# One load-and-store queue, two orders: store, load per tile against two stores, two loads per pair of tiles, with a new start and end

## The chip, the cores and the metric

One core of one Trainium2 chip. The metric is the device time of the kernel in microseconds (us). The time before was 4976.5 us, the median of three runs (4975.0 to 4977.91). The record lists a granted clock of 1.00 for every run and the state of all of them as fast.

Two kinds of engine appear below. VectorE and ScalarE compute. The 16 DMA engines move data. In the trace of the kernel before, a whole transfer is 128 packets of 64 KiB (32,512 for 254 whole transfers) and leaves 16 landings, up to 5.7 us apart, of which I take one for each DMA engine; the kernel waits for all 16 (near 2496 us the last came at 2496.28 and VectorE's first reduce began at 2496.36), so a transfer counts here as landed with the last. "Fastest" and "slowest" are the first and the last of these 16 to end a given transfer. The kernel allocates its tiles in SBUF, and a scratch tile that no transfer touches in PSUM.

## The reference

```python
# x: (256, 256, 4096) float32, eps = 1e-5
mean = np.mean(x, axis=2, keepdims=True)
var = np.var(x, axis=2, keepdims=True)
return ((x - mean) / np.sqrt(var + eps)).astype(np.float32)
```

That is 65,536 independent rows of 4,096 numbers, 1.07 GB in and 1.07 GB out. The inputs are drawn from a normal distribution, so they are nearly normalised already. A kernel that only copies x to out therefore passes the tolerance of the comparison.

## The kernel before

A tile is 128 partitions with 4 rows each: 8.39 MB per transfer, 128 tiles, three buffers. All transfers go through one queue (q1 alone on the page, with 37,152 packets), fed by SyncE in program order.

```python
    P, K, BUFS, C = 128, 4, 3, 64
    X = [pool.tile([P, K, d], fp32, name=f"x{s}") for s in range(BUFS)]
    ...
    def take(engine, sem, count):
        engine.wait_ge(sem, count)
        engine.sem_clear(sem)
    ...
    def store(s, k, dst):                      # waits until the tile is computed
        take(S, done[s], k)
        S.dma_start(out=dst, in_=X[s][:, :k, :]).then_inc(stored[s], 16)

    def load(s, k, src):                       # waits until the buffer is stored
        take(S, stored[s], 16)
        S.dma_start(out=X[s][:, :k, :], in_=src).then_inc(loaded[s], 16)
    ...
            def _(sync):
                ...
                load(0, K, x_t[0])
                load(1, K, x_t[1])
                with S.Fori(0, rounds * BUFS, BUFS) as i:
                    for s in range(BUFS):
                        store(s, K, out_t[...i + s...])              # cut: the slice arithmetic
                        load((s + 2) % BUFS, K, x_t[...i + s + 2...])
                # cut: the last tiles; the last one is loaded and stored as two halves of 2 rows
```

Per row, VectorE reduces (mean), ScalarE squares with a running sum (variance), and the two share the work of applying scale and bias. All of a tile's rows must be through before its store is issued.

## Time and profile before

The prediction below shows the page, the stretches and the chain of this kernel. What else the argument needs:

| | before |
|---|---|
| median time, first 3 runs | 4976.5 us |
| span of the profiled execution | 4973.1 us |
| VectorE busy, ScalarE busy | 68%, 52% |
| last landing | 4971.72 us |
| slowest DMA engine, per transfer, 300-2300 us, 2500-4800 us | 19.369 us, 19.337 us |
| slowest behind fastest, near 2400 us, near 4650 us | 5.7 us, 4.9 us |

Two views of the kernel before, to be set against the changed one. First the long stretches (start:end, length, VectorE, ScalarE, POOL, clock, DMA share, GB/s):

```profile
300.00:2300.00 2000.00, 1369.43 (x982) 1049.92 (x604) 0.00 (x0) 1.00 1.00 434
2500.00:4800.00 2300.00, 1584.18 (x1137) 1210.90 (x695) 0.00 (x0) 1.00 1.00 434
```

Then the DMA issues (what, engine, count, KB each, median us from issue to landing), and the spread of that time for the stores' line:

```profile
x<-in_x_dram SPq DMA_DIRECT2D x127, 49.1
out_dram<-x SPq DMA_DIRECT2D x127, 30.4
```

```profile
DMA to landing us min/median/max: 13.8/30.4/35.1
```

A transfer takes 19.3 us. A store that lands 30.4 us after its issue was issued some 11 us before the transfer ahead of it was through. This is the reserve that keeps the queue fed; it matters below. I call it the store's **margin**: from the issue of the store to the moment at which a DMA engine ends the transfer before it. It is shorter on the fastest engine (about 6 us) than on the slowest (about 11 us), by the 5 to 6 us that lie between them.

### The profile page before, as it was taken

To read this page: it belongs to the slowest core of one execution; us is meant where nothing else is said; L and a number is where in the kernel's file an instruction comes from. 1 tells how busy PE (TensorE), PEld (TensorE's weight loads), DVE (VectorE), ACT (ScalarE), POOL (GpSimd) and SP (SyncE) were. 2 spreads that over 40 slices of the span, in tenths; PEclk is the share of its full clock that TensorE was granted. 3 is DMA by queue.
4 is the path that set the end of the run, shared out by engine and by line. 5 is a ranking of instruction groups with operands and counts; after the bars stand their busy time and mean duration, and the time that the engine had idled before them with its cause. 6 is when DMAs were issued, how large, how long until landed. Compare 5 with 4: busy or idle time off the path is not lost.

```text
span 4973.1 us, 6421 instructions
## 1 busy us (share of the span) xinstructions
DVE 3396.3 (68%) x2436; ACT 2599.6 (52%) x1493; POOL 0.2 (0%) x4
## 2 busy tenths in 40 slices
DVE  6666666677667776676666776677766766677766
ACT  5455554455545555455545555455554555455545
POOL 0000000000000000000000000000000000000000
DMA  9999999999999999999999999999999999999999
GB/s 380 434 432 432 434 431 434 433 434 434 435 434 434 433 435 434 434 434 433 435 431 438 431 436 433 434 434 433 435 432 436 432 436 431 433 435 432 434 434 411
DMA packets 37155, 2147.52 MB, mean 432 GB/s; under 512 B 4128, under 2 KB 4128, under 8 KB 4128
## 3 DMA queue, kind: packets, MB, share of 16 engines
q1 hardware_dynamic: 37152, 2147.50, 99.8%
q14 instruction: 3, 0.02, 0.0%
HBM read 1073.74 MB, written 1073.74 MB: 432 GB/s over the span
## 4 chain that ended last, share of the span: by engine, by line
DMA 74%; DVE 17%; ACT 7%; issue 1%; another core or an unknown queue 1%; SPq 0%; ACTq 0%; DVEq 0%
DMA x<-in_x_dram 42%; DMA out_dram<-x 32%; DVE part L87 16%; ACT junk L127 3%; ACT x L135 3%; DVE nsum L89 1%; DVE nmean L91 1%; DVE x L107 0%; ACTq L153 0%; SPq L141 0%; ACT std L132 0%; SPq L145 0%; ACTq L69 0%; ACT L119 0%
## 5 line engine op out<-in xcount | busy, mean ns | idle before, releaser
L87 DVE TENSOR_REDUCE part<-x 128x64 f32<-128x4096 f32 x512 | 2258.8, 4412 | 1438.2 <-DMA x<-in_x_dram 1438.2
L127 ACT ACTIVATE junk<-x,nmean 128x4096 f32<-128x4096 f32 x512 | 1882.2, 3676 | 2337.3 <-DVE nmean L91 2337.3
L107 DVE TENSOR_SCALAR x<-x,rstd,nbias 128x4096 f32<-128x4096 f32 x383 | 912.5, 2411 | 37.7 <-DVE nbias L99 16.0
L135 ACT ACTIVATE x<-x,nbias,rstd 128x4096 f32<-128x4096 f32 x129 | 488.5, 3787 | 0.0
L89 DVE TENSOR_REDUCE nsum<-part 128x1 f32<-128x64 f32 x512 | 112.7, 220 | 17.7
L127 ACT ACTIVATION_READ_ACCUMULATOR junk<-x,nmean 128x1 f32 x512 | 95.5, 187 | 0.0
L91 DVE TENSOR_SCALAR nmean<-nsum 128x1 f32<-128x1 f32 x512 | 78.7, 154 | 17.5
L97 DVE RECIPROCAL rstd<-std 128x3 f32<-128x3 f32 (+1 forms) x258 | 42.0, 163 | 39.9 <-ACT std L119 31.5
L127 ACT ACT_TABLE_LOAD x41 | 52.6, 1283 | 2.0 <-DVE eps_tile L177 1.2
L119 ACT ACT_TABLE_LOAD x41 | 52.6, 1283 | 0.7
L99 DVE TENSOR_TENSOR nbias<-nmean,rstd 128x3 f32<-128x3 f32 (+1 forms) x258 | 41.5, 161 | 8.9
L132 ACT ACTIVATE std<-ss,eps_tile 128x1 f32<-128x1 f32 x129 | 38.0, 295 | 15.0
L119 ACT ACTIVATE std<-ss,eps_tile 128x3 f32<-128x3 f32 x129 | 38.2, 296 | 3.3
L177 DVE MEMSET eps_tile<- 128x1 f32 x1 | 0.1, 59 | 1.0 <-SPq L152 1.0
L208 POOL MEMSET const-bfloat16-1.0<- 128x1 bf16 x1 | 0.1, 101 | 0.0
L208 POOL MEMSET const-uint8-127<- 128x1 uint8 x1 | 0.1, 101 | 0.0
L208 POOL MEMSET const-float32-0.0<- 128x1 f32 x1 | 0.1, 98 | 0.2 <-issue 0.2
L208 POOL MEMSET const-float32-1.0<- 128x1 f32 x1 | 0.1, 98 | 0.0
## 6 DMA issues: line engine op xcount, KB each, us to landing
x<-in_x_dram SPq DMA_DIRECT2D x2, 4096.0 KB, 29.6
out_dram<-x SPq DMA_DIRECT2D x2, 4096.0 KB, 17.4
x<-in_x_dram SPq DMA_DIRECT2D x127, 49.1
out_dram<-x SPq DMA_DIRECT2D x127, 30.4
```

Source lines behind the costliest of these rows:

```text
L87: mine(V.tensor_reduce(out=part[s][:, r, :], in_=row, axis=AX.X, op=ALU.add))
L89: mine(V.tensor_reduce(out=nsum[s][:, c], in_=part[s][:, r, :], axis=AX.X, op=ALU.add, negate=True))
L91: V.tensor_scalar_mul(out=nmean[s][:, c], in0=nsum[s][:, c], scalar1=1.0 / d).then_inc(means, 1)
L97: mine(V.reciprocal(out=rstd[s][:, c], in_=std[s][:, c]))
L99: mine(V.tensor_mul(out=nbias[s][:, c], in0=nmean[s][:, c], in1=rstd[s][:, c]))
L107: V.tensor_scalar(out=x[:, r, :], in0=x[:, r, :], scalar1=rstd[s][:, c], scalar2=nbias[s][:, c], op0=ALU.mult, op1=ALU.add,).then_inc(done ...
L119: A.activation(out=std[s][:, : k - 1], in_=ss[s][:, : k - 1], func=AF.Sqrt, bias=eps_tile, scale=1.0 / d).then_inc(stds, 1)
L127: A.activation(out=junk, in_=x[:, r, :], func=AF.Square, bias=nmean[s][:, c], scale=1.0, accum_out=ss[s][:, c]).then_inc(own_a, 1)
L132: A.activation(out=std[s][:, c], in_=ss[s][:, c], func=AF.Sqrt, bias=eps_tile, scale=1.0 / d).then_inc(stds, 1)
L135: A.activation(out=x[:, k - 2, :], in_=x[:, k - 2, :], func=AF.Identity, bias=nbias[s][:, c], scale=rstd[s][:, c]).then_inc(done[s], 1)
L177: V.memset(eps_tile, eps).then_inc(ready, 1)
L208: nc = _bacc.Bacc("TRN2", target_bir_lowering=False, num_devices=1)
```

## The change

The intent: issue more loads before the first store, so that no hole is left at the start; halve the changes of direction in the queue; and have the last tile's data early. The first tile is loaded, computed and stored in halves. The last tile is loaded whole, computed and stored in halves.

```diff
-                load(0, K, x_t[0])
-                load(1, K, x_t[1])
-                with S.Fori(0, rounds * BUFS, BUFS) as i:
-                    for s in range(BUFS):
-                        store(s, K, ...)
-                        load((s + 2) % BUFS, K, ...)
+                for h in range(2):
+                    r = half_of(h)
+                    S.dma_start(out=X[0][:, r, :], in_=x_t[0][:, r, :]).then_inc(second(loaded, 0, h), 16)
+                load(1, 1, wait=False)
+                load(2, 2, wait=False)
+                store_half(0, 0, 0)
+                store_half(0, 0, 1)
+                store(1, 1)
+                take(S, stored[BUFS], 16)
+                load(0, 3)
+                load(1, 4)
+                with S.Fori(0, 20) as i:
+                    for j in range(L0, L0 + 6, 2):
+                        for t in (j, j + 1):
+                            store(t % BUFS, (t, 6, 20, i))
+                        for t in (j + 3, j + 4):
+                            load(t % BUFS, (t, 6, 20, i))
+                for op, t in ((store, 122), (store, 123), (load, 125), (store, 124), (load, 126), (load, 127),
+                              (store, 125), (store, 126)):
+                    op(t % BUFS, t)
+                store_half(last % BUFS, last, 0)
+                store_half(last % BUFS, last, 1)
```

Cut: the row offset that lets the compute functions work on half a tile, and one more semaphore of each kind for second halves.

More of the change, by code (lines that the diff above doesn't have):

```diff
@@ L35 @@
     out_t = out_flat.rearrange("(t p k) d -> t p k d", p=P, k=K)
+    assert ntiles == 128
     half = K // 2
-    h0 = n - P * K
-    x_h = x_flat[h0:n, :].rearrange("(h p k) d -> h p k d", p=P, k=half)
-    out_h = out_flat[h0:n, :].rearrange("(h p k) d -> h p k d", p=P, k=half)
     pool = ctx.enter_context(tc.tile_pool(name="pool", bufs=1))
@@ L53 @@
     )
-    loaded = [nc.alloc_semaphore(f"loaded{s}") for s in range(BUFS)]
-    stored = [nc.alloc_semaphore(f"stored{s}") for s in range(BUFS)]
+    loaded = [nc.alloc_semaphore(f"loaded{s}") for s in range(BUFS + 1)]
+    stored = [nc.alloc_semaphore(f"stored{s}") for s in range(BUFS + 1)]
     own_v = nc.alloc_semaphore("own_v")
@@ L63 @@
     scaled = nc.alloc_semaphore("scaled")
-    done = [nc.alloc_semaphore(f"done{s}") for s in range(BUFS)]
+    done = [nc.alloc_semaphore(f"done{s}") for s in range(BUFS + 1)]
     ready = nc.alloc_semaphore("ready")
@@ L71, with vector_tile @@
     V, A, S = nc.vector, nc.scalar, nc.sync
-    def vector_tile(s, k):
+    def vector_tile(s, r0=0, k=K, ld=None, dn=None):
         x = X[s]
+        ld = loaded[s] if ld is None else ld
+        dn = done[s] if dn is None else dn
         own = 0
@@ L81, in mine @@
             return instruction.then_inc(own_v, 1)
-        take(V, loaded[s], 16)
-        for r in range(k):
+        if ld:
+            take(V, ld, 16)
+        for r in range(r0, r0 + k):
             c = slice(r, r + 1)
@@ L91, in vector_tile @@
             V.tensor_scalar_mul(out=nmean[s][:, c], in0=nsum[s][:, c], scalar1=1.0 / d).then_inc(means, 1)
-        for i, c in enumerate((slice(0, k - 1), slice(k - 1, k))):
+        last = r0 + k - 1
+        for i, c in enumerate((slice(r0, last), slice(last, last + 1))):
             if i == 0:
@@ L104, in vector_tile @@
                 take(V, own_v, own)
-            for r in range(0, k - 2) if i == 0 else (k - 1,):
+            for r in range(r0, last - 1) if i == 0 else (last,):
                 c = slice(r, r + 1)
@@ L109, in vector_tile, with scalar_tile @@
                     op0=ALU.mult, op1=ALU.add,
-                ).then_inc(done[s], 1)
-    def scalar_tile(s, k):
+                ).then_inc(dn, 1)
+    def scalar_tile(s, r0=0, k=K, ld=None, dn=None):
         x = X[s]
-        for r in range(k):
+        dn = done[s] if dn is None else dn
+        last = r0 + k - 1
+        for r in range(r0, r0 + k):
             c = slice(r, r + 1)
-            if r == k - 1:
+            if r == last:
                 A.wait_ge(own_a, k - 1)
                 A.activation(
-                    out=std[s][:, : k - 1], in_=ss[s][:, : k - 1], func=AF.Sqrt, bias=eps_tile, scale=1.0 / d
+                    out=std[s][:, r0:last], in_=ss[s][:, r0:last], func=AF.Sqrt, bias=eps_tile, scale=1.0 / d
                 ).then_inc(stds, 1)
@@ L123, in scalar_tile @@
             else:
-                if r:
-                    A.wait_ge(own_a, r)
-                A.wait_ge(means, r + 1)
+                if r > r0:
+                    A.wait_ge(own_a, r - r0)
+                A.wait_ge(means, r - r0 + 1)
             A.activation(
@@ L130, in scalar_tile, with rows_of, store, load @@
         take(A, own_a, k)
-        c = slice(k - 1, k)
+        c = slice(last, last + 1)
         A.activation(out=std[s][:, c], in_=ss[s][:, c], func=AF.Sqrt, bias=eps_tile, scale=1.0 / d).then_inc(stds, 1)
-        c = slice(k - 2, k - 1)
+        c = slice(last - 1, last)
         take(A, scaled, 1)
         A.activation(
-            out=x[:, k - 2, :], in_=x[:, k - 2, :], func=AF.Identity, bias=nbias[s][:, c], scale=rstd[s][:, c]
-        ).then_inc(done[s], 1)
-    def store(s, k, dst):
-        take(S, done[s], k)
-        S.dma_start(out=dst, in_=X[s][:, :k, :]).then_inc(stored[s], 16)
-    def load(s, k, src):
-        take(S, stored[s], 16)
-        S.dma_start(out=X[s][:, :k, :], in_=src).then_inc(loaded[s], 16)
-    rounds = (ntiles - 4) // BUFS
-    tail = [(t % BUFS, K, x_t[t], out_t[t]) for t in range(rounds * BUFS, ntiles - 1)]
-    tail += [((ntiles - 1 + h) % BUFS, half, x_h[h], out_h[h]) for h in range(2)]
+            out=x[:, last - 1, :], in_=x[:, last - 1, :], func=AF.Identity, bias=nbias[s][:, c], scale=rstd[s][:, c]
+        ).then_inc(dn, 1)
+    def rows_of(ap, t):
+        if isinstance(t, int):
+            return ap[t]
+        first, period, count, i = t
+        ap = ap[first : first + period * (count - 1) + 1 : period]
+        return ap[bass.ds(i, 1)].rearrange("o p k d -> p (o k) d")
+    def store(s, t):
+        take(S, done[s], K)
+        S.dma_start(out=rows_of(out_t, t), in_=X[s][:, :, :]).then_inc(stored[s], 16)
+    def load(s, t, wait=True):
+        if wait:
+            take(S, stored[s], 16)
+        S.dma_start(out=X[s][:, :, :], in_=rows_of(x_t, t)).then_inc(loaded[s], 16)
+    def half_of(h):
+        return slice(h * half, (h + 1) * half)
+    def second(sems, s, h):
+        return sems[BUFS] if h else sems[s]
+    def store_half(s, t, h):
+        r = half_of(h)
+        take(S, second(done, s, h), half)
+        S.dma_start(out=out_t[t][:, r, :], in_=X[s][:, r, :]).then_inc(second(stored, s, h), 16)
+    def halves(tile_fn, s, first):
+        for h in range(2):
+            ld = second(loaded, s, h) if first or h == 0 else False
+            tile_fn(s, h * half, half, ld, second(done, s, h))
+    last = ntiles - 1
+    rounds = (ntiles - 5) // BUFS
+    L0 = 2
     with tc.tile_critical():
@@ L156, in _ @@
             def _(sync):
-                for s in range(BUFS):
-                    S.sem_inc(stored[s], 16)
-                load(0, K, x_t[0])
-                load(1, K, x_t[1])
-                with S.Fori(0, rounds * BUFS, BUFS) as i:
-                    for s in range(BUFS):
-                        store(s, K, out_t[bass.ds(i + s, 1)].rearrange("o p k d -> p (o k) d"))
-                        load((s + 2) % BUFS, K, x_t[bass.ds(i + s + 2, 1)].rearrange("o p k d -> p (o k) d"))
-                todo = tail[2:]
-                for t, (s, k, _, dst) in enumerate(tail):
-                    if t == len(tail) - 3:
-                        load(*todo.pop(0)[:3])
-                    store(s, k, dst)
-                    if todo:
-                        load(*todo.pop(0)[:3])
-                for s in range(BUFS):
+                for h in range(2):
+                    r = half_of(h)
+                    S.dma_start(out=X[0][:, r, :], in_=x_t[0][:, r, :]).then_inc(second(loaded, 0, h), 16)
[18 more added lines that the diff above has]
+                store_half(last % BUFS, last, 1)
+                for s in ((last - 2) % BUFS, (last - 1) % BUFS, last % BUFS, BUFS):
                     take(S, stored[s], 16)
@@ L177, in _ @@
                 V.memset(eps_tile, eps).then_inc(ready, 1)
+                halves(vector_tile, 0, True)
+                vector_tile(1)
                 with V.Fori(0, rounds) as i:
-                    for s in range(BUFS):
-                        vector_tile(s, K)
-                for s, k, _, _ in tail:
-                    vector_tile(s, k)
+                    for j in range(BUFS):
+                        vector_tile((L0 + j) % BUFS)
+                vector_tile((last - 2) % BUFS)
+                vector_tile((last - 1) % BUFS)
+                halves(vector_tile, last % BUFS, False)
             @block.scalar
@@ L186, in _ @@
                 take(A, ready, 1)
+                halves(scalar_tile, 0, True)
+                scalar_tile(1)
                 with A.Fori(0, rounds) as i:
-                    for s in range(BUFS):
-                        scalar_tile(s, K)
-                for s, k, _, _ in tail:
-                    scalar_tile(s, k)
+                    for j in range(BUFS):
+                        scalar_tile((L0 + j) % BUFS)
+                scalar_tile((last - 2) % BUFS)
+                scalar_tile((last - 1) % BUFS)
+                halves(scalar_tile, last % BUFS, False)
 _INS = ['x', 'eps']
```

## The prediction

- A paragraph of general statements about transfers. What the trace shows of them: loads 0 and 1, issued together, landed at 23.18 and 42.51 us, 19.33 us apart, and in mid-run the 16 landings of a transfer lay 5.7 us apart.
- "I count 1 us" at the direction changes: that 1 us is an estimate of mine between 0 and 3 us. The trace shows long packets of 2.6 us per engine between 300 and 1000 us, while the spread grew from 1.6 to 5.6 us, and of 0.3 us between 1000 and 2500 us.
- In rival 1, "Against both" means: against a gain and against a loss from fewer changes.

> **What bounds the kernel now.** I read the page's DMA rows first, then stretches of time, then the chain that ended last, then single landings in the trace.
>
> The page, 40 slices of 124.3 us each, and the share of the 16 DMA engines' time in which the one data queue had packets under way:
>
> ```profile
> GB/s 380 434 432 432 434 431 434 433 434 434 435 434 434 433 435 434 434 434 433 435 431 438 431 436 433 434 434 433 435 432 436 432 436 431 433 435 432 434 434 411
> q1 hardware_dynamic: 37152, 2147.50, 99.8%
> ```
>
> Every slice but the first and the last moves 431 to 438 GB/s. VectorE is busy 68% and ScalarE 52%, so neither is the bound. Only the two outer slices leave anything. The stretches (start:end, length, VectorE, ScalarE, POOL, clock, DMA share, GB/s) say where:
>
> ```profile
> core 0: us, DVE busy (x) ACT busy (x) POOL busy (x), PEclk, DMA share, GB/s
> 20.00:40.00 20.00, 16.48 (x10) 9.79 (x5) 0.00 (x0) 1.00 1.05 455
> 40.00:44.00 4.00, 2.98 (x6) 3.97 (x5) 0.00 (x0) 1.00 0.00 0
> 44.00:48.00 4.00, 4.00 (x2) 3.88 (x4) 0.00 (x0) 1.00 0.00 0
> 48.00:52.00 4.00, 3.82 (x5) 3.02 (x1) 0.00 (x0) 1.00 0.00 0
> 52.00:56.00 4.00, 3.93 (x3) 0.00 (x0) 0.00 (x0) 1.00 1.23 524
> 2000.00:2400.00 400.00, 278.82 (x201) 214.35 (x125) 0.00 (x0) 1.00 1.00 434
> 4950.00:4960.00 10.00, 2.85 (x4) 7.75 (x4) 0.00 (x0) 1.00 0.85 367
> 4960.00:4973.10 13.10, 0.00 (x0) 0.00 (x0) 0.00 (x0) 1.00 0.66 285
> ```
>
> (A packet counts where it starts, so short stretches exceed 1.) In the middle the engines are at 1.00. There is one hole, 40 to 52 us: loads 0 and 1 have landed, store 0 cannot go before tile 0 is computed, and load 2 sits behind store 0 in SyncE's program order. The chain says the same (start, length, what):
>
> ```profile
> 1.27 21.96 DMA x<-in_x_dram
> ...
> 23.32 4.43 DVE part L87
> ...
> 51.58 0.36 SPq L141
> ...
> 52.20 41.85 DMA x<-in_x_dram
> ```
>
> Tile 0 lands at 23.2 us, its store is issued at 51.58. Later in the run the chain is a DMA all the time it is not computing, and the computing lies beside other transfers:
>
> ```profile
> 2447.03 49.25 DMA x<-in_x_dram
> ...
> 2496.36 4.43 DVE part L87
> ...
> 2523.79 38.97 DMA out_dram<-x
> ```
>
> Load issue to landing is 49 us while one transfer takes 19.3: it queues behind others. From landing (2496.28) to the store's issue (2523.79) is 27.5 us of computing; I call it the tile's latency. VectorE's total wait for loads:
>
> ```profile
> DVE part L87 <- DMA x<-in_x_dram: 1438.2, 127, 22.2
> ```
>
> The trace's packet records give the floor. 32,512 packets of 64 KiB and 512 of 32 KiB; 30,342 of the former take 2418 ns, for loads and stores alike. Eight per engine and transfer are 19.34 us. Landings by semaphore: in mid-run the fastest engine finishes a transfer every 19.32 us, whichever its direction, and the slowest follows 5.7 us behind it (at its first transfer 0.5 us). Packets beyond 2418 ns add 9 us per engine over the run, nearly all in the last or first packets of a transfer, and after a third of the run they are rare. From 94.01 us on (load 2 landed) to the last landing at 4971.72, the slowest engine did 252 transfers: 19.356 us each.
>
> [...]
>
> **The change, part by part.** Bytes, packets and VectorE and ScalarE work stay the same, but for the first and last tile, computed in two halves (a few small instructions more, beside DMA).
>
> *Head.* Loads 0 (two halves), 1 and 2 are issued at once, without waits. First half lands at about 13.5 us, second at 23.2, load 1 at 42.5, load 2 at 61.8. Computing the halves: two rows of reduce (4.42 + 0.22 + 0.15 each), two squares with read-out (3.85 each), one table load (1.28), two square roots (0.3), two applications beside each other (3.79 and 2.41): first half done near 32 us, second near 48.5, tile 1 near 75 (27.2 us after the second half on VectorE). The queue runs load 2 until 61.8, then store 0's halves until 81.2, then store 1, issued near 76: 4 us ahead. The hole is gone. What it cost: 9.9 us from landing 42.51 to the store's first packet at 52.39; store 0 then took 20.9 us and load 2 20.7, against 19.36, because packets after the restart and at the first change of direction ran 0.5 to 1.8 us over: 1.6 + 1.3. Sum 12.7 us.
>
> *Steady state.* The queue runs S(a) S(a+1) L(a+3) L(a+4). Take period 77.4 us, with stores of the last pair at 0 to 38.7, L(a+1) to 58.0, L(a+2) to 77.4. Tile a landed at 0 and waited for a-1 to be computed: done at 35; S(a) needed at 77.4. Tile a+1 lands at 58.0, its store is issued at 85.5 and is needed when S(a) ends: 96.7 on the slowest engine, 91 on the fastest. With 0.8 us from issue to first packet, slack is 10 or 4.6 us. L(a+3) needs S(a) landed (96.7) and is wanted at 116; L(a+4) likewise 19 us ahead. So no engine runs dry: gain 0, loss 0, for 128 tiles.
>
> *Direction changes* halve. Were the 6 us of long packets after the head to halve too, 3 us would go[...]. I count 1 us.
>
> *Tail.* The stretches show 0.85 and 0.66, which looks like some 6 us. But on the slowest engine the last four landings are at 4932.86, 4952.31, 4962.04 and 4971.72: 19.45, 9.73 and 9.68 apart, a full transfer and two halves back to back. Only faster engines idle. The early last load is therefore worth 0 here; it is needed so that the new order leaves no hole.
>
> Sum: 4976.5 - 12.7 - 1 = 4963 us, 0.3% faster. The other way round: 23.2 to the first landing + 255 x 19.356 + 1.4 to the end = 4960.4 span, + 3.4 between span (4973.1) and median time = 4963.8, before the 1 us for directions.
>
> **Rivals.**
> (1) Long runs of one direction change the rate.[...] Against both: 2418 ns for either direction, 19.33 us for the one load-after-load, and three stores in a row at the end at the usual rate. If every change costs 0.3 us more or less than I think, 128 changes fewer make 38 us, -0.8% or +0.8%: 4925 or 5000.
> (2) A wait takes the hole's place in each pair: S(a+1) comes late. For: its slack on the fast engines is only 4.6 us. Against: the slowest engine has 10[...]. To lose 2% (99 us) each of 63 pairs must idle 1.6 us on the slowest engine, so the store must be 12 us later than worked out.
> (3) The head's hole is refilled later, because store 1 is late or load 3 issues late: 4 us of slack. Then 4966 to 4976.
> (4) The tail counts after all: up to 3 us more.
>
> **Range and chances.** The floor is 256 x 19.32 us + start and end (2.3 + 1.4 + 3.4) = 4953. Ahead of it lie only the spread and drift of the engines, 5 to 11 us. Range 4955 to 4972. Over 2% faster would need shorter packets: 1%. Over 2% slower needs rival 1 or 2 at its worst: 1.5%.
>
> **What would show it.** No stretch with DMA share near 0 between 20 and 100 us, and 434 GB/s in the first slice but for some 15 us. The middle stays at 1.00 and 434. Load issue to landing falls from 49 to about 39 us; stores split into some at 30 and some at 57. VectorE's wait for loads stays near 1440 us in total, in half as many waits, up to 23 us each. Last landing near 4958. I am wrong if the middle leaves 434 GB/s, if its landings, counted per transfer, move from 19.32 to 19.36 us, or if a hole recurs in every pair.

## The result, and the profile after

Six runs of the changed kernel and six of the kernel before on the same chip: 4977.4 us (4974.47 to 4982.33) against 4975.7 us (4975.0 to 4977.91). The ratio is 1.0004, 95% interval 0.9991 to 1.0017: the same. Such ratios are the mean time of one kernel's fast runs over that of the other's of the same rounds, so not quite the ratio of the medians quoted. The 4963 us of the prediction and its range of 4955 to 4972 were missed.

The page after, in 40 slices of 124.4 us, and the share of the data queue:

```profile
GB/s 422 437 430 436 431 436 430 436 431 436 431 436 431 436 431 435 433 431 436 432 436 431 432 434 431 431 430 434 433 430 432 430 435 431 430 430 431 432 435 397
q1 hardware_dynamic: 37296, 2147.50, 100.0%
```

The first slice rises from 380 to 422 and the share from 99.8% to 100.0%. In the second half of the line there is a slight sag: values of 430 to 432 are common where the kernel before mostly has 432 to 436. The stretches, with the columns as in the prediction:

```profile
20.00:40.00 20.00, 15.02 (x15) 15.10 (x11) 0.00 (x0) 1.00 1.03 446
40.00:44.00 4.00, 0.27 (x3) 3.80 (x2) 0.00 (x0) 1.00 1.21 524
44.00:48.00 4.00, 3.32 (x4) 3.92 (x2) 0.00 (x0) 1.00 0.61 262
48.00:52.00 4.00, 3.96 (x2) 0.06 (x1) 0.00 (x0) 1.00 1.21 524
52.00:56.00 4.00, 3.97 (x2) 3.78 (x2) 0.00 (x0) 1.00 1.06 459
300.00:2300.00 2000.00, 1359.51 (x977) 999.00 (x566) 0.00 (x0) 1.00 1.00 433
2500.00:4800.00 2300.00, 1557.64 (x1121) 1146.08 (x647) 0.00 (x0) 1.00 1.00 432
```

Three stretches of DMA share 0.00 have become 1.21, 0.61 and 1.21, whose mean is 1.01: the hole is gone. But the long stretches, at share 1.00 as before, move 433 and 432 GB/s instead of 434. A share of 1.00 says that packets were under way all the time, not that each took its usual time. VectorE's waits for loads (total us, times, longest), the DMA issues, and the stores' time from issue to landing in the changed kernel:

```profile
DVE part L89 <- DMA x<-in_x_dram: 1473.4, 64, 24.4
```

```profile
x<-in_x_dram SPq DMA_DIRECT2D x127, 38.5
out_dram<-x SPq DMA_DIRECT2D x126, 37.3
```

```profile
DMA to landing us min/median/max: 27.3/37.3/58.4
```

VectorE waits as long as before (1438.2 us) in half as many waits, loads wait less in the queue (38.5 instead of 49.1), and stores fall into a group near 30 and one near 57. All this is the pair order at work as intended.

Where the time went can be read from the landing records, counted per transfer:

| slowest DMA engine | before | after |
|---|---|---|
| four full transfers landed at | 94.0 us | 82.5 us |
| from there 252 more, each | 19.356 us | 19.412 us |
| last landing | 4971.72 us | 4974.33 us |
| per transfer, 300-2300 us | 19.369 us | 19.386 us |
| per transfer, 2500-4800 us | 19.337 us | 19.427 us |
| slowest behind fastest, near 2400 / 4650 us | 5.7 / 4.9 us | 8.3 / 9.0 us |
| margin of the tight store, slowest / fastest, near 4500 us | 11.2 / 6.3 us | 11.4 / 2.4 us |

The start gained 94.0 - 82.5 = 11.5 us. The loop gave back 252 x 0.056 = 14.1 us. Of these, (2300 / 19.4 = 119 transfers) x 0.090 = 10.7 us lie between 2500 and 4800 us. In pair order the tight store is the second of a pair, since the first is long in the queue.

The packet records say in which packets the loop lost. I summed what packets took beyond their usual 2418 ns, per DMA engine, from 300 to 4900 us: 4.6 us before, 16.1 us after. From 2500 to 4700 us, the packets next to a change from loads to stores are over by 28 ns per change and engine before, and by 326 ns after; at changes from stores to loads it is at most 1 ns before and 58 ns after. Per transfer that makes 28/2 = 14 ns before (a change to stores with every second transfer) and (326 + 58)/4 = 96 ns after. The difference, 82 ns, is about what the landings show: 79 ns on the fastest engine (19.343 to 19.422) and 90 on the slowest.

So half the changes of direction are gone, and each change from loads to stores that is left took some twelve times the excess (326 ns against 28).

One thing about these long packets matters for all that follows. Between 2500 and 4700 us, those at the changes from loads to stores begin 10 to 22 us before the tight store is issued (13 to 22 us in e13 below), and they are mostly the last packets of the load. At the boundary between the two stores of a pair, where the tight store itself is awaited, packets are over by 3 ns in all. So a small margin and long packets go together, but the late store doesn't lengthen its own packets or those just ahead of it.

### The profile page after: what moved, and what is told of

It reads as the page before. It is cut to its first block, busy times and chain, and to the rows that moved or that the text cites. A ratio compares the mean times of both kernels' runs of the same rounds, so it can differ in the third digit from the quotient of the medians.

```text
span 4975.7 us, 6254 instructions
## 1 busy us (share of the span) xinstructions
DVE 3384.4 (68%) x2439; ACT 2505.6 (50%) x1416; POOL 0.2 (0%) x4
## 4 chain that ended last, share of the span: by engine, by line
DMA 49%; DVE 25%; another core or an unknown queue 14%; ACT 10%; issue 1%; SPq 1%; ACTq 0%; DVEq 0%
DMA x<-in_x_dram 48%; DVE part L89 23%; ACT junk L132 5%; ACT x L140 5%; DVE nsum L91 1%; DVE nmean L93 1%; DMA out_dram<-x 1%; SPq L154 0%; DVE x L110 0%; ACT std L137 0%; SPq L159 0%; ACTq L182 0%; ACTq L68 0%; SPq L68 0%
## 5 line engine op out<-in xcount | busy, mean ns | idle before, releaser
L89 DVE TENSOR_REDUCE part<-x 128x64 f32<-128x4096 f32 x512 | 2258.0, 4410 | 1473.4 <-DMA x<-in_x_dram 1473.4
L100 DVE RECIPROCAL rstd<-std 128x1 f32<-128x1 f32 (+1 forms) x260 | 41.8, 161 | 17.2 <-ACT std L137 16.5
L102 DVE TENSOR_TENSOR nbias<-nmean,rstd 128x1 f32<-128x1 f32 (+1 forms) x260 | 41.6, 160 | 8.9
L124 ACT ACTIVATE std<-ss,eps_tile 128x3 f32<-128x3 f32 (+1 forms) x130 | 38.5, 296 | 4.2
## 6 DMA issues: line engine op xcount, KB each, us to landing
x<-in_x_dram SPq DMA_DIRECT2D x127, 38.5
```

The lines of the kernel that those rows point to most:

```text
L89: mine(V.tensor_reduce(out=part[s][:, r, :], in_=row, axis=AX.X, op=ALU.add))
L100: mine(V.reciprocal(out=rstd[s][:, c], in_=std[s][:, c]))
L102: mine(V.tensor_mul(out=nbias[s][:, c], in0=nmean[s][:, c], in1=rstd[s][:, c]))
L124: A.activation(out=std[s][:, r0:last], in_=ss[s][:, r0:last], func=AF.Sqrt, bias=eps_tile, scale=1.0 / d).then_inc(stds, 1)
```

## The experiments

The theories, with the letters that the expectations use:

- **A**: the pair order itself costs; the memory or the engines dislike longer runs of one direction.
- **B**: the filled start costs; without the hole the DMA engines begin in another state, whatever the order of the loop.
- **C**: the second store of a pair comes too late for the fast DMA engines, that is, the margin. First I took it as a plain count with the spread of before; later (**C2**) with the spread that grows, so that about one packet (2.4 us) of margin is left on the fastest engine.
- **D**: VectorE's and ScalarE's accesses to SBUF disturb the transfers; as **D2**, those at the moment of the change from loads to stores.

Each run was compared with the kernel before on the same chip. The sets ran on three chips; the kernel before had medians of 4975.28 to 4976.51 us on them, so runs of different sets are set against each other only for differences well above 1 us. A summary, read from each trace like the table above ("long" is the excess of packets per DMA engine, 300 to 4900 us; the spread is the slowest behind the fastest near 2400 and 4650 us; the margins are the late ones):

| run | median us | slowest, us per transfer, early / late | spread, mid / late | margin, slowest / fastest | long us |
|---|---|---|---|---|---|
| before | 4975.7 | 19.369 / 19.337 | 5.7 / 4.9 | 11.2 / 6.3 | 4.6 |
| after | 4977.4 | 19.386 / 19.427 | 8.3 / 9.0 | 11.4 / 2.4 | 16.1 |
| e1 (a long execution) | 4968.83 | 19.518 / 19.565 | 9.8 / 9.7 | 11.6 / 1.6 | 45.0 |
| e2 | 4986.55 | 19.390 / 19.411 | 8.2 / 9.2 | 11.6 / 2.5 | 13.9 |
| e3 | 4962.3 | 19.402 / 19.323 | 9.2 / 9.6 | 37.9 / 28.4 | 3.8 |
| e4 | 4960.22 | 19.388 / 19.320 | 5.4 / 5.6 | 38.5 / 32.9 | 5.6 |
| e5 | 4962.58 | 19.372 / 19.329 | 5.7 / 6.6 | 13.2 / 7.0 | 2.8 |
| e6 | 4959.95 | 19.342 / 19.319 | 6.4 / 6.4 | 13.1 / 6.7 | 1.5 |
| e7 | 5261.83 | 19.442 / 19.428 | 13.7 / 16.4 | 37.9 / 21.9 | 12.4 |
| e9 | 4965.9 | 19.357 / 19.366 | 6.1 / 10.7 | 38 / 28 | 2.7 |
| e10 | 4970.31 | 19.363 / 19.389 | 7.2 / 14.5 | 38 / 24 | 3.0 |
| e11 | 4967.39 | 19.357 / 19.368 | 5.9 / 11.5 | 38 / 27 | 2.2 |
| e12 | 5577.53 | 19.392 / 19.396 | 9.7 / 16.3 | 38 / 22 | 5.1 |
| e13 | 5003.72 | 19.484 / 19.427 | 4.3 / 3.7 | 6.3 / 2.5 | 29.7 |
| e14 | 4967.84 | 19.384 / 19.353 | 9.5 / 13.1 | 16.0 / 3.2 | 4.2 |
| e15 | 4967.52 | 19.331 / 19.372 | 5.2 / 11.5 | 16.0 / 4.9 | 1.2 |
| e16 | 4981.14 | 19.389 / 19.427 | 11.8 / 14.2 | 16.1 / 1.9 | 15.9 |
| e17 | 4975.36 | 19.370 / 19.391 | 9.3 / 13.8 | 16.1 / 2.4 | 6.6 |

e8 and e18 have transfers of another size and are told in their places. The times of e7 and e12 are the ends of a compute loop, not of the transfers.

### e1 and e2: one part at a time

e1 keeps the new start and end and puts the old order back into the loop:

```diff
-                load(1, 4)
-                    for j in range(L0, L0 + 6, 2):
-                        for t in (j, j + 1):
-                            store(t % BUFS, (t, 6, 20, i))
-                        for t in (j + 3, j + 4):
-                            load(t % BUFS, (t, 6, 20, i))
+                    for j in range(L0, L0 + 6):
+                        store(j % BUFS, (j, 6, 20, i))
+                        load((j + 2) % BUFS, (j + 2, 6, 20, i))
```

> The changed kernel with its head (tile 0 in halves, loads 0 to 2 at once) and its tail (last tile loaded early), but the old order of one store, then one load, in the loop. Theory A (the order of pairs in the loop lengthens packets at each change from load to store, and that eats the 12 us of the head): the loop runs as before, 19.36 us per transfer on the slowest engine, and the head's 12 us stay: 4963 to 4966 us, long packets add about 7 to 9 us per engine in place of 19. Rival B (whatever fills the hole at the head starts the engines in another pattern, and the long packets come from that): 4975 to 4979 us as in the changed kernel, packets long by 17 us or more per engine.

Measured: six runs fell into two groups: 4963.09, 4963.81, 4965.34 and 4972.33, and 5007.84 and 5010.65. The ratio over all is 0.9996 (0.9971 to 1.0022). The profile is of the 5010.65 one. Its long stretch late in the run:

```profile
2500.00:4800.00 2300.00, 1563.51 (x1121) 1148.98 (x649) 0.00 (x0) 1.00 1.00 429
```

Here 12 DMA engines ended their transfers within 0.3 to 0.7 us of each other and four followed 7 to 10 us later, and long packets came to 45.0 us. What follows: the new start with the old loop can give the 4963 us that I had predicted for the whole change, which is 12 us below the runs of before beside it (4975.6). So the gain of the start is real and can be kept. But the same program also runs at 5010 us. The pair order isn't needed for a slow loop, against A; B is true in part, as a filled start can lead to a slow loop. In this slow loop the long packets lie more at changes from stores to loads (late in the run about 310 ns per change and engine, against about 130 at the others), so they are not tied to one direction of change.

e2 is the reverse, the old start with the pair loop:

```diff
-                for h in range(2):
-                    S.dma_start(out=X[0][:, r, :], in_=x_t[0][:, r, :]).then_inc(second(loaded, 0, h), 16)
+                S.dma_start(out=X[0][:, :, :], in_=x_t[0]).then_inc(loaded[0], 16)
                 load(1, 1, wait=False)
+                store(0, 0)
                 load(2, 2, wait=False)
```

> The changed kernel with the old head (tile 0 whole, load 2 behind store 0), so with the hole of 10 us, and the new order in the loop and the new tail. Theory A (the loop's order costs): hole and loop loss add up: 4986 to 4990 us. Rival B (the filled head is what spoils the loop): as before, 4974 to 4978 us.

Measured: 4986.55 us (4985.57 to 4988.7), ratio 1.0021 (1.0008 to 1.0034). This is what theory A had forecast: the pair loop costs 4986.55 - 4975.6 = 11 us with the old start. The new start takes off 4986.55 - 4977.4 = 9 us of that (these two from different sets). The excess in the packets begins near 2586 us, when the margin on the fastest engine has fallen to 2.5 us. The slowest engine, however, takes 19.39 us per transfer between 1600 and 2600 us and keeps 19.39 to 19.40 up to 4100 us, so reaching the small margin changed little for it at first. Still, the filled start isn't needed for the loss, against B as the only cause.

### e3 and e4: the transfers alone

Both take the computing away: the store waits for the load only. Their outputs are wrong, which doesn't matter for the times. e3 has the pair order, e4 the old one.

```diff
     def store(s, t):
-        take(S, done[s], K)
+        take(S, loaded[s], 16)
# and the blocks of VectorE and ScalarE removed, first and last tile whole
```

> No computing at all (wrong on purpose: out = x), the same loads and stores in the new order of pairs. If long packets come of the DMA order alone (theory A1), the slowest engine takes 19.40 us per transfer as in the changed kernel and packets are long by 15 us or more per engine; about 4972 to 4978 us. If they come of VectorE and ScalarE using SBUF while loads change to stores (theory A2), they vanish: 19.32 per transfer, about 4950 to 4956 us.

> As the run before, in the old order of one store, one load. Theory A1: shorter than the pairs' copy by 10 us or more, 4955 to 4966 us. Theory A2: the same as the pairs' copy within 4 us, 4950 to 4956 us.

Measured: 4962.3 us (4960.74 to 4963.65) in pairs and 4960.22 us (4959.7 to 4963.3) alternating. The late stretch of e3 and of e4:

```profile
2500.00:4800.00 2300.00, 0.00 (x0) 1.00 1.00 434
```

```profile
2500.00:4800.00 2300.00, 0.00 (x0) 1.00 1.00 434
```

Both times are above the 4950 to 4956 us that A2 had forecast, but the late pace of 19.32 us and the absence of long packets are A2's. The pair order costs about 2 us here, in ranges that overlap. Theory A, with the order alone as the cause, falls. Against e3 the changed kernel loses nothing up to about 1840 us: in both, the slowest engine takes 19.36 to 19.46 us per transfer while the engines spread. From about 2340 us on, e3 is flat at 19.32 with its engines 9.3 to 9.6 us apart, and the changed kernel goes on at 19.43: 0.104 us x 119 transfers = 12.4 us of the 15 us between 4977.4 and 4962.3. So in e3 a spread of 9.3 to 9.6 us did no harm at a margin of 28.4 us.

### e5 and e6: the wait of the computing, without its SBUF accesses

The copy again, but each store waits until ScalarE has made seven passes over PSUM after the load's landing, some 25.5 us. Only the transfers touch the tiles in SBUF.

```diff
+                def gate(s):
+                    take(A, loaded[s], 16)
+                    for q in range(7):
+                        A.activation(out=junk, in_=junk, func=AF.Identity, scale=1.0).then_inc(own_a, 1)
+                        ...                                    # wait for it
+                    A.sem_inc(done[s], 1)
```

> The copy in pairs (4962 us without computing), but each store waits for seven ScalarE passes over PSUM after its tile has landed, some 27 us as in the real kernel, without touching the tiles in SBUF. Wrong on purpose (out = x). Theory C (the store's late release: only about 10 us of slack, so that an engine lagging by about 10 us makes the others run dry and start together again, and packets at load-to-store changes stay long): 4970 to 4982 us, long packets 15 us or more per engine, in the whole run. Theory D (VectorE and ScalarE using SBUF beside the transfers lengthens packets): 4960 to 4964 us as the plain copy.

> As the run before, with one store, one load in turn (4960 us without the wait). Theory C: like the run with the old loop and the filled head, either about 4963 or up to 5010 us, different from execution to execution; the lag of the slowest engine near 10 us in the long ones. Theory D: 4959 to 4964 us in all.

Measured: 4962.58 us (4961.94 to 4967.51) in pairs, 4959.95 us (4959.42 to 4960.73) alternating. Neither loses against its copy; between the two orders lie 2.6 us. The margin on the fastest engine stays near 7 us in both. So a wait of 25.5 us in itself cost nothing here (4962.58 against 4962.3 us, 4959.95 against 4960.22), and C as I had first put it falls. It was 2 us shorter than the real latency of 27.5 us, which left C with other numbers open; e13 takes that up.

### e7: SBUF accesses without the wait

The copy in pairs, while VectorE and ScalarE work on tiles of their own:

```diff
+                with V.Fori(0, 360) as i:
+                    # 4 reduces and 3 applications over 2048 columns of its own tile, each awaited
+                with A.Fori(0, 680) as i:
+                    # 4 squares and 1 copy over 1024 columns of its own tile
```

> The copy in pairs with VectorE and ScalarE busy in SBUF for nearly the whole time on tiles of their own, which no transfer waits for. Wrong on purpose (out = x). Theory C: 4960 to 4964 us as the plain copy. Theory D: 4970 us or more, at least what the changed kernel lost.

Measured: 5261.83 us, ratio 1.0573. That figure is useless: I had made ScalarE's loop too long, and it ended last. The transfers' last landing was at 4979.8 us, against 4960.4 in e3's trace. So SBUF work alone can cost 19 us, as D had forecast. But the picture is another one: a single DMA engine is slower throughout, at 19.43 us per transfer. The fastest engine runs at 19.32 and the spread grows to 16.4 us near 2850 us, where the changed kernel holds 9 us. There the fastest engine's margin for the loads has come down to 2.4 us; from then on it takes 19.43 us as well and the spread stays. So in e7 the spread stopped growing at a margin of 2.4 us, one packet's time, for a load and not a store, while the slowest engine's pace stays as it was. It doesn't show how the changed kernel lost: there the slowest engine itself slows late, from 19.34 us (1840 to 2340 us) to 19.42 (2340 to 4840).

### e8: smaller tiles, more of them

A correct kernel with tiles of 2 rows, six buffers, loads four ahead, and the order of before:

```diff
-    K = 4
-    BUFS = 3
+    K = 2
+    BUFS = 6
+    AHEAD = 4
```

> Correct kernel with tiles of two rows in six buffers in place of four rows in three, one store and one load in turn, loads four tiles ahead: the tile's latency falls from 27 to some 17 us and the slack of a store grows from 10 to about 60 us; no hole at the head. Theory C: the engines spread as in the copy and stay so: 4958 to 4963 us in every execution. Theory D (same work in SBUF): it loses as the changed kernel does, 4970 to 4985 us.

Measured: 4975.25 us (4974.97 to 4975.74), ratio 0.9998 (0.9984 to 1.0011). Margins of 40 and 31 us, and only 0.4 us of long packets: the loss at direction changes is gone. Another takes its place. A half-size transfer takes 9.681 us when nothing disturbs it, so two take 2 x 9.681 - 19.319 = 0.043 us longer than one whole. Over 256 whole transfers that is 11 us, about as much as was gained. One engine also falls behind from 2400 us on (9.699 us per transfer late in the run), some 4 us more. The time lies in D's range and misses C's 4958 to 4963 us; the landings give these two other reasons for it, so the run decides neither way.

### e9 to e12: when, and which engine's, SBUF work

Copies in pairs with a burst of VectorE and ScalarE work on their own tiles, started by SyncE once per pair. In e9 it starts just before the pair's second store is issued, so that it lies on the change from loads to stores. In e10 it starts two transfers later, at the pair's first load. Cut: a second pair of semaphores, so that the signal isn't given twice before it is taken.

```diff
                     store(j % BUFS, (j, 6, 20, i))
                     take(S, loaded[(j + 1) % BUFS], 16)
+                    S.sem_inc(go_v, 1)      # e9: here.  e10: ahead of the first load of the pair
+                    S.sem_inc(go_a, 1)
                     store((j + 1) % BUFS, (j + 1, 6, 20, i), False)
```

> The copy in pairs with one burst of some 26 us of VectorE and ScalarE work in SBUF per pair, on tiles of their own that no transfer waits for, begun when the first load of a pair has landed: so it runs while the engines change from loads to stores. In the changed kernel VectorE and ScalarE are busy at that change (packets long by 330 ns per engine and change), in the kernel before they are idle at it (28 ns). Theory D2 (SBUF work at the moment of the change from loads to stores lengthens the packets): the last landing 10 us or more later than the plain copy's 4960.4, long packets 12 us or more per engine; 4970 us or more. Rival (the moment does not matter, only the amount of SBUF work): as the burst elsewhere, within 3 us.

> The same burst, begun when the first store of a pair has landed, so that it covers the second store and the change from stores to loads and is over before the next change from loads to stores. Theory D2: as the plain copy, 4960 to 4964 us, long packets 5 to 8 us per engine. Rival: as the burst at the change.

Measured: 4965.9 us (4965.7 to 4967.38) at the change, 4970.31 us (4969.58 to 4972.26) elsewhere; long packets 2.7 and 3.0 us. The burst at the change is not the dearer one, so D2 falls, as far as copies with 38 us of margin can tell. Both again have one DMA engine that falls steadily behind; the spread is 12 and 16 us in the end.

e11 lets VectorE alone work freely, e12 ScalarE alone:

```diff
+                with V.Fori(0, 345) as i:   # e11: 4 reduces, 3 applications, no ScalarE
+                with A.Fori(0, 850) as i:   # e12: 4 squares, no VectorE work
```

> The copy in pairs with VectorE alone busy in SBUF all the time. If VectorE's SBUF work is what slows the transfers, last landing some 19 us later than the plain copy's, as with both engines (4979.8 against 4960.4); if it is ScalarE's, 4960 to 4964 us.

> The copy in pairs with ScalarE alone reading SBUF all the time (writing PSUM). If ScalarE's reads slow the transfers, some 4980 us; if VectorE's, 4960 to 4964 us.

Measured: e11 4967.39 us (4966.99 to 4968.02), last landing 4964.8. e12's time of 5577.53 us is again the end of ScalarE's own loop, too long by my mistake; its last landing is at 4971.2. Against 4960.4 in e3's trace, either engine's work cost 4 to 11 us, through one slow DMA engine (19.368 and 19.396 us per transfer late in the run, against 19.323 in e3); neither of the two outcomes forecast (some 4980 us, or 4960 to 4964) came. In e12 the fastest engine's margin for the loads is down to 2.7 us near 3900 us, and its pace goes from 19.32 to 19.40 there, as in e7. The ratios of this set have wide intervals (0.9953, 0.9888 to 1.0017, for e9), because two runs of the kernel before took 5018.66 and 5020.35 us; see the end of this section.

### e13: less margin, no SBUF work

e5 with nine PSUM passes instead of seven, some 32 us:

```diff
-                    for q in range(7):
+                    for q in range(9):
```

> The copy in pairs with nine ScalarE passes over PSUM (some 32 us) in place of seven between a tile's landing and its store: no SBUF work at all; the slowest engine still has some 6 us to spare, so a count of waits alone forecasts no loss (4960 to 4963 us, as with seven). C2: the fastest engine's margin falls to 2.5 us when it is only 3.5 us ahead; the spread is held there, packets stay long through the run, 15 us or more per engine, 4972 us or more. D3: 4960 to 4964 us.

Measured: 5003.72 us (5002.25 to 5005.47), ratio 1.0055 (1.0039 to 1.007): 41 us more than e5. A stretch at the start and the two long ones, and the stores' time from issue to landing; first e5, then e13, with a stretch at its end too:

```profile
82.00:92.00 10.00, 0.00 (x0) 9.90 (x4) 0.00 (x0) 1.00 0.97 419
300.00:2300.00 2000.00, 0.00 (x0) 1284.49 (x361) 0.00 (x0) 1.00 1.00 434
2500.00:4800.00 2300.00, 0.00 (x0) 1483.81 (x416) 0.00 (x0) 1.00 1.00 434
```

```profile
DMA to landing us min/median/max: 26.2/33.1/57.8
```

```profile
82.00:92.00 10.00, 0.00 (x0) 9.68 (x3) 0.00 (x0) 1.00 0.25 105
300.00:2300.00 2000.00, 0.00 (x0) 1656.31 (x465) 0.00 (x0) 1.00 1.00 431
2500.00:4800.00 2300.00, 0.00 (x0) 1895.87 (x533) 0.00 (x0) 1.00 1.00 432
4974.00:4982.00 8.00, 0.00 (x0) 7.25 (x3) 0.00 (x0) 1.00 0.00 0
```

```profile
DMA to landing us min/median/max: 20.8/26.6/53.0
```

The shares of 0.25 and 0.00 are two holes, outside the loop. The second store of the very first pair and the last store of all are late, since ScalarE makes its passes for one tile after the other. By the landings on the slowest engine they cost 9.1 us (the fifth transfer lands at 111.02 us, in e5 at 101.89) and 8.7 us (28.03 us between the last two landings, in e5 19.32). In the traces e13 ends 43.5 us later than e5, so some 26 us are left for the loop, where the share is 1.00 and 431 to 432 GB/s are moved, as in the changed kernel. There the tight stores still have 5.9 to 7.2 us of margin on the slowest DMA engine, and 2.5 (at least 1.4) on the fastest, so by a plain count nothing should wait. Packets are nevertheless over by 29.7 us per engine, against 2.8 in e5, a difference of 27 us that fits the loop's loss. As no engine but ScalarE works, and in PSUM only, such a loss needs no SBUF work. The later issue of the stores brought it about, before any engine was empty by that count (2.5 us left). ScalarE is busier too (83% of the early stretch, 64% in e5), but e12, with ScalarE at work 90% of the time and 38 us of margin, has only 5.1 us of long packets. C2 is supported.

### e14 and e15: more margin in the real kernel

Three of four rows are computed, so a tile is ready earlier. The result is wrong. e14 is the changed kernel, e15 is e1, each so cut:

```diff
-    def vector_tile(s, r0=0, k=K, ld=None, dn=None):
+    def vector_tile(s, r0=0, k=K - 1, ld=None, dn=None):
-    def scalar_tile(s, r0=0, k=K, ld=None, dn=None):
+    def scalar_tile(s, r0=0, k=K - 1, ld=None, dn=None):
-        take(S, done[s], K)
+        take(S, done[s], K - 1)
```

> The changed kernel, but of the four rows of a tile only three are computed (the fourth is stored as it came, wrong on purpose; tile 0 and the last are whole): tile latency 22.5 in place of 27.5 us, so 5 us more margin, with three quarters of the SBUF work. C2: the margin of the fastest engine stays over 2.5 us, 4959 to 4965 us. D3: three quarters of the loss remains, 4970 us or more.

> The same with the old order in the loop (head and tail of the changed kernel), whose whole version ran from 4963 to 5010 us. C2: 4958 to 4964 us in every execution, none near 5010. D3: still some executions of 4972 us or more.

Measured: e14 4967.84 us (4967.38 to 4969.18), ratio 0.9983 (0.997 to 0.9997); e15 4967.52 us (4966.73 to 4968.24), the same ratio. Both are 3 us above the top of what I expected. The long packets fall from 16.1 to 4.2 us in pairs; alternating, none of five runs was near 5010. The 5 to 7 us that are left against the copies (4962.3 and 4960.22) show as one DMA engine falling behind, as in e7 and e9 to e12. One caveat: with a row less there is also a quarter less SBUF work, so these two alone don't tell margin from SBUF work. e13 shows that margin alone can do it, not how much of it is margin here.

### e16 and e17: a shorter correct kernel, a miss

To gain margin without giving up rows, VectorE takes mean and variance of three rows with one statistics instruction per 512 columns, and ScalarE takes the fourth row whole. The latency of a tile falls to 22.7 us. e16 has the old loop order, e17 the pairs; both issue three loads first.

```diff
-            mine(V.tensor_reduce(out=part[s][:, r, :], in_=row, axis=AX.X, op=ALU.add))
+            for c in range(8):
+                mine(V.bn_stats(out=stats[s][:, r, c, :], in_=x[:, r, c * 512 : (c + 1) * 512]), c == 7)
+            mine(V.bn_aggr(out=mv[s][:, r, :], in_=stats[s][:, r, :, :].rearrange("p c f -> p (c f)")))
```

> A correct kernel with a shorter tile latency: VectorE takes mean and variance of three rows in one pass each, ScalarE those of the fourth, each applies two rows; some 21 us in place of 27.5, so the slowest engine's margin is some 17 us. Loads 0 to 2 at once, last tile loaded early, one store and one load in turn. C2: 4960 to 4968 us in every execution (one engine 0.05 us per transfer slower than the rest, as in the kernels with three rows, may cost up to 6 us of it). If the margin is not the cause: 4970 to 5010 us.

> The same with the new order of two stores, then two loads. C2: as the one before within 3 us, 4960 to 4968 us, so that the order no longer matters. If the order itself costs: 8 us or more above the one before.

Measured: e16 4981.14 us (4980.35 to 4983.09), ratio 1.0011 (0.9998 to 1.0025); e17 4975.36 us (4973.03 to 4977.18), ratio 0.9999 (0.9985 to 1.0012). Both expectations were missed. The slowest engine has a margin of 16 us. But in e16 one single DMA engine is slow from about 1600 us on, at 19.42 us per transfer, and the spread reaches 14 us. So the fastest engine's margin comes down to 1.9 us near 2800 us all the same. The slowest engine ran at 19.42 before that point and after it: reaching the margin changed nothing for it here. In e16, then, a spread that grew to 14.2 us ate the added margin, and the 1.9 us left on the fastest engine did not set the slowest one's pace.

### e18: margin by smaller tiles

A correct kernel with 170 tiles of 3 rows and one of 2, four buffers, loads three ahead, the order and the instructions of before:

```diff
-    K = 4
-    BUFS = 3
+    K = 3
+    BUFS = 4
+    AHEAD = 3
```

> A correct kernel with tiles of three rows in four buffers (170 tiles and one of two rows), loads 0 to 2 issued at once, one store and one load in turn, loads three tiles ahead, statistics as in the kernel before. Tile latency 22.5 us as in the kernels with three rows computed, margin of the slowest engine about 35 us. If a margin beyond the spread keeps the gain: no long packets held to the end and 4963 to 4970 us in every execution (floor of the copy 4960, some 4 us for 342 transfers in place of 256 at 0.04 us each, up to 6 us for the one slower engine). If the margin is not what matters: 4972 us or more, or executions near 5010.

Measured: 4966.4 us (4971.1, 4966.09, 4965.07, 4966.4, 4969.17) against 4975.28 us beside it, ratio 0.9983 (0.9969 to 0.9996). One of the five is 1 us above the 4970 that I had expected "in every execution". This is the lowest median of a correct kernel that I found, 9 us or 0.2% below the kernel before. Its late stretch and VectorE's wait for loads:

```profile
2500.00:4800.00 2300.00, 1552.84 (x1189) 1287.16 (x750) 0.00 (x0) 1.00 1.00 434
```

```profile
DVE part L87 <- DMA x<-in_x_dram: 1205.7, 168, 18.0
```

434 GB/s to the end, margins of 35.3 and 22.5 us, 1.2 us of long packets, though the engines are 13 us apart late in the run. A transfer of 3 rows takes 14.523 us early and 14.527 late on the slowest engine, 14.50 on the fastest. The order is still store, load.

**The kernel before, seen often.** With the six runs of the first comparison it ran 61 times in all. Three runs took 5013.07, 5018.66 and 5020.35 us at a granted clock of 1.00; the others lie close to 4976. No profile fell on one of the three. They resemble e1's long runs in size; whether they have the same cause isn't known.

## Why the prediction was right or wrong

- **Head: right.** I had 12.7 us from the hole and two slow transfers; 11.5 us were measured, with no stretch near share 0 between 20 and 100 us. e1's runs at 4963 show the gain in the time, too.
- **Tail: right.** I had said 0. The last landings are 4954.96, 4964.66 and 4974.33 us, 9.70 and 9.67 apart: half transfers back to back on the slowest engine, as before.
- **Queue depths: right.** 38.5 us for loads (39 predicted), stores near 30 and near 57, VectorE's wait 1473.4 us in 64 waits up to 24.4 (1440, half as many, 23).
- **Direction changes, "I count 1 us" of gain: wrong in sign.** Halving their number was right, but their price was taken from a loop in which they cost 28 ns; it became 326 ns. (That long packets are rare after a third of the run was a loose reading: 2.3 of the 8.8 us in the kernel before come later.)
- **Steady state, "So no engine runs dry: gain 0, loss 0": this is the step that failed.** It lost 14.1 us by the landings. Its term was the slack, "10 or 4.6 us". For the slowest engine it was right (11.4 us). For the fastest it rested on the spread of 5.7 us read from the kernel before, and the spread grew to 9 us in the new loop: 2.4 us were left, the time of one packet. And the conclusion from slack to "loss 0" was wrong on its own: e13 loses some 26 us in the loop with a margin that by the count is never used up, at 2.5 us on the fastest engine.

In the traces the sum closes: the prediction had -12.7 - 1 = -13.7 us, the last landing moved by -11.5 + 14.1 = +2.6 us, and the gap of 16.3 us is 1.2 (head) + 1 (changes) + 14.1 (loop). Rival 2, a late second store, was the right place to look. I had dismissed it for the 10 us of slack on the slowest engine and for an assumption about waits on fast engines that no trace had shown. By the margins of 2.4 us on the fastest engine and 11.4 on the slowest no engine had to wait for the store; packets at the change from loads to stores got longer (326 ns against 28), and the slowest engine lost as well as the fastest: from 2340 to 4840 us the slowest takes 19.42 us per transfer, against 19.32 in e3. That these packets run 10 to 22 us before the late store is issued was no part of the rival, nor of C2. My own signal for being wrong, landings per transfer going from 19.32 to 19.36 us, came true and more: 19.43.

What is shown: the order by itself cost 2 to 3 us (e3 with e4, e5 with e6); a wait of the computing's kind cost nothing with 13 us of margin (e5, e6) and some 26 us in the loop with 6 (e13), without any SBUF work; with more margin the long packets fell from 16.1 us to 4.2 (e14, where there is less SBUF work too), and to 1.2 in e18; the head's gain can be had (e1's short runs from 4963.09 us on, e18's 4966.4). That the small margin makes up the whole of the changed kernel's 14.1 us is argued from these, not shown: a slower engine beside VectorE and ScalarE work, as in e16, may have a part in it. What stays open:

- Why packets lengthened at changes of direction when the margin was small though not used up (326 ns at 2.4 us on the fastest engine), and why 10 to 22 us before the late store was issued. That the two go together is measured; the mechanism isn't.
- What sets the spread. Two copies differ by order (9.6 and 5.6 us), but with a gate in between both have 6.4 to 6.6, and e1 reached 9.7 in the old order.
- Why one DMA engine is slower by 0.04 to 0.11 us per transfer in runs with VectorE or ScalarE work (e7, e9 to e12, e14 to e17), and hardly in the kernel before, where the spread went from 5.7 to 4.9 us.
- Why the slowest engine keeps its pace in e7, e12 and e16 when the fastest engine's margin is down to about one packet (2.4, 2.7 and 1.9 us), and slows in the changed kernel and e13 (2.4 and 2.5 us).
- Why e1, and rarely the kernel before, falls into runs some 40 us longer.

## What to carry to other kernels

Where one queue is the bound, ask of each store how long before its turn it is issued, count that for the fastest DMA engine, and do not take the spread between engines from the old loop. Here the spread went from 5.7 and 4.9 us to 8.3 and 9.0 with the new loop, and the margin on the fastest engine from 6.3 us to 2.4, the time of one packet. A share of 1.00 didn't show the loss here (1.00 before and after, 2500 to 4800 us); landings per transfer did (19.337 us before, 19.427 after). Smaller tiles with more buffers bought margin, 35.3 us on the slowest engine in e18 and 40 in e8 against 11.2 before, at 0.043 us for each added transfer in e8, and three rows in four buffers had here a lower median (4966.4 us) than any order of stores and loads with whole tiles that computed all rows.
